# Output projection: x's and v's products in one item, m1's and m2's late additions with y, and tile halves normalised on VectorE and ScalarE

## The chip, the cores and the metric

The kernel runs on one core of a Trainium2 chip. The metric is the device time of one execution in microseconds; several runs are given by their median, lowest and highest. The profile is one execution taken by the hardware profiler. In its rows PE is TensorE (PEld its weight loads), DVE is VectorE, ACT is ScalarE, POOL is GpSimd and SP the engine that issues most DMAs; L1160 is line 1160 of the kernel. A time like 574.58 is counted in microseconds from the start of the span.

## The reference, cut to what matters

Two layers, each a token mixer of three gated branches, one output projection, a residual addition with a layer norm, and then a SwiGLU feed-forward block (FFN) with a second residual and norm. The changed code is the output projection with its norm (`ln1`), and the norm's step that is also used between the two layers (`ln2` of the first):

```
    for l in range(DEPTH):                        # 2
        h = jnp.einsum('bsd,de->bse', x, w_in[l])
        ...
        mix = jnp.einsum('bsd,de->bse', merged, w_out[l])
        x = _layer_norm(DEEPNORM_ALPHA * x + mix, ln1_g[l], ln1_b[l])

        u = jnp.einsum('bsd,df->bsf', x, w_ffn_in[l])
        u_gate, u_up = jnp.split(u, 2, axis=-1)
        ffn = jnp.einsum('bsf,fd->bsd', jax.nn.silu(u_gate) * u_up, w_ffn_out[l])
        x = _layer_norm(DEEPNORM_ALPHA * x + ffn, ln2_g[l], ln2_b[l])
```

x is 512 rows by 1024 columns, w_out 1024 by 1024, everything in float32.

## The kernel before

**Numbers as pairs.** A float32 value is carried as a high and a low part (names that end in `h` and `l`, or `wh` and `wl` for weights). One product is three matmuls (`mm3`, L122 to L124): high by high, high by low, low by high. ACT makes the high part with a cast (L106, or L282 for a weight block), DVE the low part with a subtraction (L112, or L283).

**Weights.** A block of weights comes by DMA into a buffer `st` (SP's queue, or POOL's at L178), is cast to `wh` by ACT (L282) and split by DVE (L283, `wl`). There are three buffers of `wh` and `wl`, and the program prepares blocks up to three ahead of the item that uses them.

**Items.** The program is a list of items `(specs, fn, groups...)`: `specs` are the weight blocks, `fn` issues the products on PE and what follows them, and each group is a list of small functions that is run between the steps of the item's `fn`. The text order of the items, and of what is prepared ahead, gives a first order; a scheduler places each engine's instructions, so the order on an engine is not quite that of the text. Each engine runs its own queue in that order, and waits where an instruction's input isn't there.

**The output projection** (`out_items`) computes the 512 x 1024 by 1024 x 1024 product by a seven-product scheme on halves: the products are named m1, m2, y, v, x, g and h, each on sums of halves of the activations (`m2h`, `s12h`, `s43h`) and on sums of blocks of the weight, which the class `Late` builds with DVE additions in place (L271, `e += d`, builds the block of h). Each product has two row tiles (`j` 0 and 1). Several products share a bank of PSUM: x, g and h go on accumulating in m1's, v in y's. So a product that goes on in a bank can start only when DVE has read what the bank held.

**Residual tiles.** The residual stands in SBUF as row tiles of 128 rows in two halves of 512 columns, `z[t][hf]`. `plus` adds a bank's contents to a half: the first time with the residual's factor (L1160), then plainly (L1162); after the last of a half come the statistics (`stats`, L489, BN_STATS). m1's and m2's additions are kept in a list `late` and run in v's item. When both halves are whole, `normalise` (L504) computes mean and variance (BN_AGGR, L506), adds eps (L508), raises to the power -1/2 on POOL (L509) and applies both to the two halves on DVE (L511).

**The transposes.** The FFN needs the normalised rows turned: PE transposes the halves into banks `px` (L529, or L520 at the layer boundary), ACT evacuates each with scale and shift (L545, to `xf`), casts it to `xTh` (L106), and DVE makes `xTl` (L112). The first FFN products (`pf`) run between them.

`normalise` is used at three places: in the out-projection of layer 0 (from about 580 us), at the layer boundary behind the first FFN (930 to 945 us) and in the out-projection of layer 1 (from about 1510 us). The end of the last layer uses another function (`finish`).

`bcast_rows` (L476) loads ln1's scale and shift rows into tiles `bc` on SP's queue; it is called by `norm_rows`, a group of x's item.

Of the kernel before, what the change touches and what calls it, by code (L numbers as in the profile page):

```python
# [12 lines left out]
F32 = mybir.dt.float32  # L13
F32R = mybir.dt.float32r
AF = mybir.ActivationFunctionType
ALU = mybir.AluOpType

P = 128
# [38 lines left out]
def trunk(ctx, tc, x_in, xT_in, w_in, ret_norm_g, da_norm_g, lq1, lk1, lq2, lk2, w_a, w_b, w_c, b_merge, w_out,  # L57
          ln1_g, ln1_b, w_ffn_in, w_ffn_out, ln2_g, ln2_b, rel, rope_ret, rope_da, decay, out):
    nc = tc.nc
    ctx.enter_context(nc.allow_low_precision("float32 operands are carried exactly as pairs of float32r"))  # L60
    cpool = ctx.enter_context(tc.tile_pool(name="cpool", bufs=1))
    small = ctx.enter_context(tc.tile_pool(name="small", bufs=6))
# [128 lines left out]
    class Chain(Halves):  # L191
# [15 lines left out]
        def x(self):  # L207
            return self.take(1, 0)
# [4 lines left out]
        def v(self):  # L213
            return self.block(self.load(1, 1))
# [147 lines left out]
    def product(acts, name, j, wt, ps=None):  # L362

        onto, sl = ps is not None, slice(P * j, P * j + P)
        ps = ps if onto else bank("pf")
        for k in range(wt.nk):
            hi, lo = acts[k].use[name]
            mm3(ps, hi[:, sl], lo[:, sl], wt.hi[:, k], wt.lo[:, k], k == 0 and not onto, k == wt.nk - 1, onto)
        return ps
# [109 lines left out]
    class Norm:  # L479
# [24 lines left out]
        def normalise(self, t):  # L504
            mv = small.tile([P, 2], F32, tag="mv", name="mv")
            nc.vector.bn_aggr(mv, self.st[t])  # L506
            rs = small.tile([P, 1], F32, tag="rs", name="rs")
            nc.vector.tensor_scalar_add(rs, mv[:, 1:2], LN_EPS)  # L508
            nc.gpsimd.tensor_tensor(rs, rs, mhalf[:, 0:1], op=ALU.pow)  # L509
            for z in self.z[t]:  # L510
                nc.vector.tensor_scalar(z, z, mv[:, 0:1], rs[:, 0:1], op0=ALU.subtract, op1=ALU.mult)  # L511

        def transposes(self, t):
            hf, j = divmod(t, 2)
# [49 lines left out]
    def between():  # L564

        if pending:
            for fn in pending.pop(0):
                fn()
# [58 lines left out]
    def layer(l):  # L627
# [7 lines left out]
        v = {}  # L635
# [64 lines left out]
        def u_rqk(dst, base, hp):  # L700
            def fn(wt):
                for j in range(2):
                    rqk_done(dst, 2 * hp + j, proj_T(xT, wt, P * j))
                    between()
            return [([wcols(base + 256 * hp, 256)], KT)], fn
# [87 lines left out]
        def s_dh(h):  # L793
            def fn():
                dhs[h] = g(name="dh")
                nc.sync.dma_start(dhs[h], decay[h])
            return fn

        def s_r1(h):
            def fn():  # L800
                dh = dhs.pop(h)
                rp[h] = triangle("rp")
                q, k = rq.pop(h), rk.pop(h)
                for b in range(3):
                    tmp = g(name="rtmp")
                    for mt in range(NT):
                        if PACK[mt][0] != b:
                            continue
                        o, w = PACK[mt][1], S - P * mt
                        ps = bank("psr")  # L810
                        msl = slice(P * mt, P * mt + P)
                        mm3(ps[:, :w], k.hi[:, msl], k.lo[:, msl], q.hi[:, P * mt:], q.lo[:, P * mt:], True, True)
                        nc.vector.tensor_mul(tmp[:, o:o + w], ps[:, :w], dh[:, :w])
                    w = PACKW[b]
                    split(rp[h][b], tmp[:, :w], cols=slice(0, w))
            return fn
# [37 lines left out]
        def s_r3(h):  # L854
            def fn():
                os_ = rps.pop(h)
                for d in range(2):
                    ps = bank("prt")
                    for nt in range(NT):
                        nc.tensor.transpose(ps[:, P * nt:P * nt + P],  # L860
                                            os_[nt // 2][:, 256 * (nt % 2) + P * d:256 * (nt % 2) + P * d + P], ident)
                    oa[2 * h + d] = Pair("oa")
                    split(oa[2 * h + d], ps, scale=v["rg"][:, d:d + 1])
            return fn
# [30 lines left out]
        def u_cqk(p):  # L895
            def fn(wt):
                cqk[p] = QK()
                cqk[p].set_q(proj_T(xT, wt, 0), -CA_DH ** -0.5)
                between()
                cqk[p].set_k(proj_T(xT, wt, P))  # L900
            return [([wcols(CQ + P * p, P), wcols(CK + P * p, P)], KT)], fn
# [173 lines left out]
        def u_gate(br, i):  # L1075
            def fn(wt):
                for j, d in enumerate(tiles(br, i)):
                    gate_done(br, d, proj_T(xT, wt, P * j), (br, i) in EARLY)
                    between()
            return [(cols_of(W, GATE + D * br, br, i), KT)], fn  # L1080
# [39 lines left out]
        def s_mleft(k):  # L1120
            def fn():
                mq[k].left(acc[k], acc[k + 4], 0.5)
            return fn

        def s_mright(k):
            def fn():
                mq[k].right(acc.pop(k), acc.pop(k + 4), 0.5)
            return fn
# [44 lines left out]
        def out_items():  # L1173

            hv = Late(w_out[l], 0, 4)
            w = {}
            late = []

            def it(name, i, hf, op, last=False, whole=False):
                def fn(wt):  # L1180
                    on = {"x": "m1", "g": "m1", "h": "m1", "v": "y"}.get(name, name)
                    for j in range(2):
                        t = 2 * i + j
                        ps = w[on, j] = product(mq, name, j, wt, w.pop((on, j), None))
                        add = functools.partial(plus, x1, t, hf, ps, op, last)
                        if name in ("m1", "m2"):
                            late.append(add)
                        else:
                            add()
                        if name == "v":  # L1190
                            for fn in late[j::2]:
                                fn()
                        if whole:
                            x1["n"].normalise(t)
                        between()
                return [getattr(hv, name)], fn

            add, sub = ALU.add, ALU.subtract
            return {"c": hv.ahead_c, "a": hv.ahead_a, "m1": it("m1", 0, 0, add), "m2": it("m2", 0, 0, add, True),
                    "y": it("y", 1, 1, add), "x": it("x", 0, 1, sub, True, True), "v": it("v", 0, 1, add), "g": it("g", 1, 1, sub, True),  # L1200
                    "h": it("h", 1, 0, add, True, True)}

        def s_turned(hf):
# [7 lines left out]
        o = out_items()  # L1211
# [15 lines left out]
        for (specs, fn), *groups in start + [  # L1227
            (w["x"], [p["a"]]), (u_gate(0, 3),), (w["g"],), (w["h"], [p["c"]]),
            (p["m1"], [s_dh(0)]), (p["y"], [], [s_r1(0)]), (p["v"], [s_dh(1)]), (p["m2"], [], [s_r1(1)]),
            (p["x"], [q["a"]]), (u_rqk(rq, RQ, 1),), (p["g"], [q["c"]]), (p["h"],),  # L1230
            (q["m1"], [], [s_r2(0)]), (q["y"], [s_r2(1)]), (u_rqk(rk, RK, 1), [], [s_r3(0)]),
            (q["v"], [s_dh(2)], [s_r3(1)]), (q["m2"], [], [s_r1(2)]), (q["x"], [s_dh(3)]), (u_cqk(0),), (q["g"], [], [s_r1(3)]), (q["h"],),
            (u_gate(2, 0), [s_r2(2)], [s_r2(3), s_r3(2)]), (u_cqk(1), [s_r3(3)] + c(0)[0], c(0)[1]),
            (u_branch(0, 0), c(1)[0] + [v_back(cv)], c(1)[1]), (u_branch(0, 1), *c(2)), (u_cqk(2), *c(3)),
            (u_branch(0, 2), *c(4)), (u_cqk(3), *c(5)), (u_branch(0, 3), *c(6)), 
            (u_dqk(0), [s_c3(5), s_c2(6)], [s_c1(7)]), (u_gate(1, 0), [s_c3(6)], [s_c2(7)]),
            (u_dqk(1), [v_back(dv), s_c3(7)] + d(0)[1]), (u_branch(1, 0), *d(1)),
            (u_gate(1, 1), [], d(2)[1]), (u_branch(1, 1), [s_d2(0)], d(3)[1]), (u_dqk(2), [s_d3(0)]),
            (u_gate(1, 2), *d(4)), (u_branch(1, 2), *d(5)), (u_dqk(3),),
            (u_gate(1, 3), *d(6)), (u_branch(1, 3), *d(7)), (u_gate(2, 1), [gates_in(2, 0), s_d4(2)], [s_d2(3)]),  # L1240
            (u_gate(2, 2), [s_d3(3)], [rows_in, s_d4(3)]),
            (u_branch(2, 0), [o["a"]], [s_mleft(0)]), (u_branch(2, 1), [], [s_mleft(1)]), (u_gate(2, 3), [s_mright(0)], [s_mright(1), o["c"]]),
            (u_branch(2, 2),), (u_branch(2, 3), [], [s_mleft(2), s_mleft(3)]),
            (o["m1"], [s_mright(2)]), (o["m2"], [s_mright(3)]), (o["y"],), (o["v"],), (o["x"], [norm_rows]),
            (o["g"], [], [s_turned(0)]), (o["h"],),
        ]:
            item(specs, fn, *groups)
# [168 lines left out]
        o, w = fout_items(0), fout_items(1)  # L1416
# [68 lines left out]
```

## Time and profile before

| | |
|---|---|
| median of 3 runs | 1878.59 us (1877.79 to 1879.77) |
| profiled execution | 1878.62 us, its span 1876.8 us |
| granted clock of TensorE | 0.999 of full speed |
| instructions | 23329 in the span |
| DMA | 302.89 MB, mean 161 GB/s |

The page gives the busy time of each engine, its share of the span and the number of instructions; PE's is 99%. The list of waits of PE names what it stood still for. A timeline row has the start, the duration, the engine, the line, the operation, output and inputs, the shape, how many instructions the row joins, and in brackets the idle time before it and what ended it. The durations of matmuls are those of a pipeline (0.39 us), while the next one starts 0.23 us later.

### The profile page before, as it was taken

The numbers are of one execution on the slowest core, as the hardware profiler recorded it, in microseconds if no ns is written. First come the engines' busy times: TensorE is split into PE (matmuls) and PEld (weight loads), VectorE is DVE, ScalarE is ACT, GpSimd is POOL, SyncE is SP. The second block draws the span as 40 slices with busy tenths as digits, with TensorE's granted clock in tenths as the row PEclk, the third lists the DMA queues.
The fourth block names the chain that finished last, engine by engine and source line by source line (L and its number), as shares of the span: only waits on it lengthen the run. The fifth ranks groups of instructions, "written<-read, shape, count | busy, mean of one in ns | idle before, by whom it ended". The sixth has DMA issues, their size and how long they took to land. (4 is left out here: it accounts for less than half of the span.)

```text
span 1876.8 us, 23329 instructions
## 1 busy us (share of the span) xinstructions
PE 1857.4 (99%) x8754; PEld 1543.6 (82%) x8754; DVE 1395.9 (74%) x2121; ACT 989.2 (53%) x1593; POOL 127.2 (7%) x149
## 2 busy tenths in 40 slices
PE   9999999999999999999999999999999999999998
PEld 7788888888887888888878888888888878888886
DVE  6777766677679777888687777567775887778886
ACT  5555555576544545554264555556665454455541
POOL 2000000000000000010020000000000001000100
PEclk9999999999999999999999999999999999999999
DMA  9585444332456577697376844433325467777871
GB/s 288 164 268 161 118 138 138 90 124 78 122 159 180 157 186 192 189 224 201 130 229 191 253 116 144 153 116 95 112 68 146 136 178 177 197 196 203 202 193 45
DMA packets 235937, 302.89 MB, mean 161 GB/s; under 512 B 8756, under 2 KB 127632, under 8 KB 235824
## 3 DMA queue, kind: packets, MB, share of 16 engines
q1 hardware_dynamic: 207600, 246.44, 40.5%
q0 software_dynamic: 28224, 54.95, 16.9%
q8 instruction: 69, 1.13, 0.2%
q14 instruction: 44, 0.36, 0.1%
HBM read 279.29 MB, written 22.07 MB: 161 GB/s over the span
## 5 line engine op out<-in xcount | busy, mean ns | idle before, releaser
L283 DVE TENSOR_TENSOR wl<-st,wh 128x2048 fp32r<-128x2048 f32 x140 | 320.1, 2289 | 118.0 <-ACT wh L282 117.4
L282 ACT CAST wh<-st 128x2048 fp32r<-128x2048 f32 x140 | 267.1, 1912 | 234.8 <-PE pf L124 114.2
L122 PE MATMUL pt<-xTh,wh 128*128 128x512 f32 x960 | 377.9, 394 | 2.0 <-ACT wh L154 1.3
L123 PE MATMUL pt<-xTl,wh 128*128 128x512 f32 x960 | 373.9, 389 | 0.2 <-DVE xTl L613 0.2
L124 PE MATMUL pt<-xTh,wl 128*128 128x512 f32 x960 | 374.1, 390 | 0.0
L155 DVE TENSOR_TENSOR wl<-st,wh 128x1024 fp32r<-128x1024 f32 (+1 forms) x188 | 200.7, 1084 | 52.3 <-ACT wh L154 38.5
L154 ACT CAST wh<-st 128x1024 fp32r<-128x1024 f32 (+1 forms) x188 | 172.6, 941 | 109.5 <-PE pt L123 56.3
L122 PEld LDWEIGHTS pt<-xTh,wh 128*128 128x128 f32 x960 | 180.5, 188 | 40.0 <-ACT wh L154 2.4
L124 PEld LDWEIGHTS pt<-xTh,wl 128*128 128x128 f32 x960 | 180.2, 188 | 38.1
L123 PEld LDWEIGHTS pt<-xTl,wh 128*128 128x128 f32 x960 | 180.4, 188 | 36.7 <-DVE xTl L613 0.5
L122 PE MATMUL pf<-wh,xTh 128*128 128x512 f32 x336 | 133.4, 398 | 1.6 <-ACT xf L545 0.5
L123 PE MATMUL pf<-wl,xTh 128*128 128x512 f32 x336 | 131.1, 390 | 0.0
L124 PE MATMUL pf<-wh,xTl 128*128 128x512 f32 x336 | 130.2, 392 | 0.0
L122 PE MATMUL pf<-wh,s43h 128*128 128x512 f32 x256 | 100.2, 392 | 1.7 <-DVE z L1162 1.7
L123 PE MATMUL pf<-wl,s12h 128*128 128x512 f32 x256 | 100.0, 391 | 1.2 <-DVE wl L283 1.2
L122 PE MATMUL pf<-wh,s12h 128*128 128x512 f32 x256 | 100.1, 394 | 0.0
L123 PE MATMUL pf<-wl,s43h 128*128 128x512 f32 x256 | 99.7, 389 | 0.0
L124 PE MATMUL pf<-wh,s12l 128*128 128x512 f32 x256 | 99.4, 390 | 0.0
L124 PE MATMUL pf<-wh,s43l 128*128 128x512 f32 x256 | 99.0, 389 | 0.0
L757 ACT COPY tc<-pf 128x512 f32<-128x512 f32 x84 | 48.5, 590 | 80.2 <-PE pf L124 75.0
L122 PEld LDWEIGHTS pf<-wh,xTh 128*128 128x128 f32 x336 | 63.1, 188 | 18.4 <-ACT xf L545 2.4
L124 PEld LDWEIGHTS pf<-wh,xTl 128*128 128x128 f32 x336 | 62.6, 188 | 15.3 <-DVE xTl L112 2.7
(328 smaller groups left out, 3661.8 us busy)
## 6 DMA issues: line engine op xcount, KB each, us to landing
st<-in_w_in SPq DMA_DIRECT2D x53, 1024.0 KB, 6.4
st<-in_w_ffn_in SPq DMA_DIRECT2D x38, 1024.0 KB, 5.5
st<-in_w_in SPq DMA_DIRECT2D x48, 512.0 KB, 4.7
st<-in_w_ffn_in POOLq DMA_DIRECT2D x20, 1024.0 KB, 10.8
st<-in_w_ffn_out SPq DMA_DIRECT2D x20, 1024.0 KB, 7.8
st<-in_w_ffn_out POOLq DMA_DIRECT2D x16, 1024.0 KB, 8.7
st<-in_w_in POOLq DMA_DIRECT2D x12, 1024.0 KB, 10.9
st<-in_w_out SPq DMA_DIRECT2D x12, 1024.0 KB, 5.1
```

The lines of the kernel that those rows point to most:

```text
L122: nc.tensor.matmul(ps, lh, rh, start=start, stop=False, skip_group_check=onto)
L123: nc.tensor.matmul(ps, lh, rl, start=False, stop=False, skip_group_check=onto)
L124: nc.tensor.matmul(ps, ll, rh, start=False, stop=stop, skip_group_check=onto)
L154: return [nc.scalar.copy(self.hi[:, a:b], self.st[:, a:b]), nc.vector.tensor_sub(self.lo[:, a:b], self.st[:, a:b], f(self.hi[:, a:b]))]
L155: nc.vector.tensor_sub(self.lo[:, a:b], self.st[:, a:b], f(self.hi[:, a:b]))]
L282: nc.scalar.copy(self.hi, st)
L283: nc.vector.tensor_sub(self.lo, st, f(self.hi))
L757: nc.scalar.copy(t[to, j], ps)
```

## The change

Three edits in the same function and one helper.

- `normalise` now computes `nb` = -mean * rs on DVE (128x1), applies the first half on ACT as rs * z + nb (an ACTIVATE with scale and bias from tiles), and the second on DVE as before.
- The list `late` runs in y's item instead of v's.
- x and v are one item, `xv`: its two weight blocks are prepared together, it issues x's products and then v's. The last product of a half on columns 512 to 1023 of rows 0 to 255 is now v's, so statistics and `normalise` follow v. `norm_rows` moves to this item's third group.

```diff
             nc.gpsimd.tensor_tensor(rs, rs, mhalf[:, 0:1], op=ALU.pow)
-            for z in self.z[t]:
-                nc.vector.tensor_scalar(z, z, mv[:, 0:1], rs[:, 0:1], op0=ALU.subtract, op1=ALU.mult)
+            nb = small.tile([P, 1], F32, tag="nb", name="nb")
+            nc.vector.scalar_tensor_tensor(nb, mv[:, 0:1], -1.0, rs, op0=ALU.mult, op1=ALU.mult)
+            z = self.z[t]
+            nc.scalar.activation(z[0], z[0], AF.Identity, scale=rs[:, 0:1], bias=nb[:, 0:1])
+            nc.vector.tensor_scalar(z[1], z[1], mv[:, 0:1], rs[:, 0:1], op0=ALU.subtract, op1=ALU.mult)
...
-                        if name == "v":
+                        if name == "y":
                             for fn in late[j::2]:
                                 fn()
...
+            x, v = it("x", 0, 1, sub)[1], it("v", 0, 1, add, True, True)[1]
+
+            def xv(wv, wx):
+                x(wx)
+                v(wv)
+
             return {"c": hv.ahead_c, "a": hv.ahead_a, "m1": it("m1", 0, 0, add), "m2": it("m2", 0, 0, add, True),
-                    "y": it("y", 1, 1, add), "x": it("x", 0, 1, sub, True, True), "v": it("v", 0, 1, add), "g": it("g", 1, 1, sub, True),
+                    "y": it("y", 1, 1, add), "xv": ([hv.v, hv.x], xv), "g": it("g", 1, 1, sub, True),
                     "h": it("h", 1, 0, add, True, True)}
...
-            (o["m1"], [s_mright(2)]), (o["m2"], [s_mright(3)]), (o["y"],), (o["v"],), (o["x"], [norm_rows]),
+            (o["m1"], [s_mright(2)]), (o["m2"], [s_mright(3)]), (o["y"],), (o["xv"], [], [], [norm_rows]),
```

In the changed kernel the lines below `normalise` stand three further: L1163 and L1165 are the additions (L1160 and L1162 before), L532 the transposes (L529), L548 the evacuation (L545). Inside it L511 is `nb`, L513 ACT's half, L514 DVE's half.

**DVE, behind v's and x's products of layer 0.** z_4786 to z_4793 are the halves of row tiles 0 to 3 (two each), pf_5108 and pf_5128 m1's banks, pf_5187 and pf_5201 y's. Before:

```order
L1160 SCALAR_TENSOR_TENSOR z_4787<-z_4787,pf_5187 128x512
L1160 SCALAR_TENSOR_TENSOR z_4789<-z_4789,pf_5201 128x512
L1162 TENSOR_TENSOR z_4787<-z_4787,pf_5108 128x512
L1162 TENSOR_TENSOR z_4789<-z_4789,pf_5128 128x512
L283 TENSOR_TENSOR wl_5253<-st_5181,wh_5252 128x2048
L489 BN_STATS bn_4802<-z_4787 128x6
L489 BN_STATS bn_4803<-z_4789 128x6
L506 BN_AGGR mv_5270<-bn_4802 128x2
L283 TENSOR_TENSOR wl_5309<-st_5306,wh_5308 128x2048
L508 TENSOR_SCALAR rs_5272<-mv_5270 128x1
L506 BN_AGGR mv_5299<-bn_4803 128x2
L1162 TENSOR_TENSOR z_4791<-z_4791,pf_5108 128x512
```

After:

```order
L1165 TENSOR_TENSOR z_4787<-z_4787,pf_5187 128x512
L271 TENSOR_TENSOR st_5148<-st_5148,st_5141 128x2048
...
L506 BN_AGGR mv_5265<-bn_4802 128x2
L489 BN_STATS bn_4803<-z_4789 128x6
L508 TENSOR_SCALAR rs_5267<-mv_5265 128x1
L283 TENSOR_TENSOR wl_5307<-st_5148,wh_5306 128x2048
L511 SCALAR_TENSOR_TENSOR nb_5270<-mv_5265,rs_5267 128x1
L514 TENSOR_SCALAR z_4787<-z_4787,mv_5265,rs_5267 128x512
L506 BN_AGGR mv_5296<-bn_4803 128x2
L283 TENSOR_TENSOR wl_5313<-st_5310,wh_5312 128x2048
L508 TENSOR_SCALAR rs_5298<-mv_5296 128x1
L1165 TENSOR_TENSOR z_4791<-z_4791,pf_5108 128x512
```

The additions that read m1's banks (pf_5108) for x stand ahead of these rows now. L271, which builds h's block, stood above the first of the rows before and now follows v's first addition; the first `nb` and DVE's half of tile 0 stand ahead of the addition that frees pf_5108 for h. Two rows are left out.

**ACT at the layer boundary.** xf_7924 to xf_7942 before and xf_7938 to xf_7956 after are the first evacuations, z_6881 is the first half of row tile 2. Before:

```order
L545 ACTIVATE xf_7930<-px_7865,colv_348 128x256
L106 CAST xTh_7928<-xf_7930 128x256
L545 ACTIVATE xf_7936<-px_7866,colv_348 128x256
L106 CAST xTh_7934<-xf_7936 128x256
L282 CAST wh_8000<-st_7998 128x2048
L545 ACTIVATE xf_7942<-px_7866,colv_348 128x256
L154 CAST wh_8005<-st_8004 128x1024
L106 CAST xTh_7940<-xf_7942 128x256
```

After:

```order
L548 ACTIVATE xf_7944<-px_7875,colv_348 128x256
L106 CAST xTh_7942<-xf_7944 128x256
L513 ACTIVATE z_6881<-z_6881,nb_7932,rs_7929 128x512
L548 ACTIVATE xf_7950<-px_7876,colv_348 128x256
L106 CAST xTh_7948<-xf_7950 128x256
L282 CAST wh_8016<-st_8014 128x2048
L548 ACTIVATE xf_7956<-px_7876,colv_348 128x256
L154 CAST wh_8021<-st_8020 128x1024
L106 CAST xTh_7954<-xf_7956 128x256
```

ACT's half of tile 2 stands between the second cast and the third evacuation; the weight cast and the fourth evacuation follow it.

## The prediction

> **What bounds the kernel now.** I read the page first, then the waits of PE, then the timelines of PE, DVE, ACT and POOL around the three places where `normalise` is called. The columns of part 1 are busy time, share of the span and count.
>
> ```profile
> PE 1857.4 (99%) x8754; PEld 1543.6 (82%) x8754; DVE 1395.9 (74%) x2121; ACT 989.2 (53%) x1593; POOL 127.2 (7%) x149
> PE pf L122 <- DVE rs L508: 2.6, 2, 1.3
> PE pf L122 <- DVE z L1162: 1.7, 2, 0.8
> PE pf L123 <- DVE wl L283: 1.2, 2, 0.6
> ```
>
> TensorE sets the time: it is busy for 99% of the span, and the change neither adds nor removes a matmul. So the change can save only time in which PE stands still, and can cost only where it makes PE stand still. The three rows of waits (total, times, longest) are the ones that lie in the out-projection, once in each layer; they sum to 5.5 us, and no forecast of a gain can be much above that. In the timeline of layer 0 they look like this (start, us, engine, then the wait in brackets):
>
> ```profile
> 570.53 0.40 PE L123 MATMUL pf<-wl,s12h 128*128 128x512 f32 x1
> 571.54 0.50 PE L123 MATMUL pf<-wl,s12h 128*128 128x512 f32 x1 [0.61 <-DVE wl L283]
> ...
> 582.47 0.39 PE L124 MATMUL pf<-wh,s12l 128*128 128x512 f32 x1
> 583.70 0.50 PE L122 MATMUL pf<-wh,s43h 128*128 128x512 f32 x1 [0.84 <-DVE z L1162]
> ...
> 586.10 0.39 PE L123 MATMUL pf<-wl,s43h 128*128 128x512 f32 x1
> 586.33 0.39 PE L124 MATMUL pf<-wh,s43l 128*128 128x512 f32 x1
> ...
> 589.05 0.39 PE L124 MATMUL pf<-wh,s43l 128*128 128x512 f32 x1
> 590.78 0.47 PE L122 MATMUL pf<-wh,m2h 128*128 128x512 f32 x1 [1.34 <-DVE rs L508]
> ```
>
> An undisturbed step from start to start is 586.33 - 586.10 = 0.23 us. The first step of item g (operand s43h) comes 1.23 us after the last of v and x, so PE loses 1.00 there; the first of h (m2h) comes after 1.73, a loss of 1.50; the early one, at 571.54, is 1.01 after its predecessor and loses 0.78.
>
> **What DVE does there** decides the first two, since g and h accumulate onto banks that DVE must have read before:
>
> ```profile
> 574.58 2.27 DVE L271 TENSOR_TENSOR st<-st 128x2048 f32<-128x2048 f32 x1
> 581.76 1.28 DVE L1160 SCALAR_TENSOR_TENSOR z<-z,pf 128x512 f32<-128x512 f32 x2 [0.83 <-PE pf L124]
> 582.96 1.28 DVE L1162 TENSOR_TENSOR z<-z,pf 128x512 f32<-128x512 f32 x2
> 584.16 2.28 DVE L283 TENSOR_TENSOR wl<-st,wh 128x2048 fp32r<-128x2048 f32 x1
> 587.66 2.24 DVE L283 TENSOR_TENSOR wl<-st,wh 128x2048 fp32r<-128x2048 f32 x1
> 589.82 0.14 DVE L508 TENSOR_SCALAR rs<-mv 128x1 f32<-128x1 f32 x1
> 590.00 0.63 DVE L1162 TENSOR_TENSOR z<-z,pf 128x512 f32<-128x512 f32 x1
> ```
>
> g starts right behind the addition of 582.96 that frees m1's first bank; h starts behind the addition of 590.00, which stood behind a subtraction of 2.24 us that nothing on PE needed yet.
>
> **Part one, the late additions with y.** By the order of the two kernels, DVE adds m1's and m2's first products at the same places in both. This edit moves nothing: 0.0.
>
> **Part two, x ahead of v in one item.** PE has already issued x's first products ahead of v's in the kernel before (s12h at 570.53), and the early wait on wl stays. What changes is DVE: the addition of x that reads m1's bank comes before v's products are done, about 574.8 instead of 582.96. g no longer waits: it starts at 582.47 + 0.23 = 582.70, a gain of 1.00 per layer. What it costs stands in the same queue: `e += d` (L271, 2.27 us), which ran at 574.58 in cover of x's and v's products, now stands behind v's first addition (580.2 to 580.8), and the block of h is built from it:
>
> - L271 ends at 580.8 + 2.27 = 583.1; ACT's cast of that block (1.91, the row of L282 in the timeline below) at 585.0; its L283 (2.28) at 587.3.
> - The power of `normalise` on POOL is issued at 585.1, beside that subtraction. These are the two forms it has in the trace, alone and beside a subtraction:
>
> ```profile
> 934.92 0.54 POOL L509 TENSOR_TENSOR rs<-rs,mhalf 128x1 f32<-128x1 f32 x1 [4.66 <-DVE rs L508]
> 943.16 1.21 DVE L155 TENSOR_TENSOR wl<-st,wh 128x1024 fp32r<-128x1024 f32 x1
> 943.39 1.39 POOL L509 TENSOR_TENSOR rs<-rs,mhalf 128x1 f32<-128x1 f32 x1 [7.93 <-DVE rs L508]
> ```
>
> It ended 0.41 behind the subtraction (943.39 + 1.39 less 943.16 + 1.21), so I let it end at 587.7. Then nb (0.16, from L1036 below) to 587.9, DVE's half tile (0.54) to 588.4, the next L283 (2.28) to 590.7, and only then the addition of g (0.68) to 591.4. h starts at 591.45, 0.67 later than before, although g ended 1.00 earlier.
>
> [...]
>
> **Part three, the halves on two engines.** Of each tile one DVE instruction goes and one ACTIVATE with two pointer operands comes, and a 128x1 instruction (nb) on DVE that must wait for POOL. For their durations (count, total and mean ns, then idle):
>
> ```profile
> L511 DVE TENSOR_SCALAR z<-z,mv,rs x24: 535/541/547, 594.6 to 1537.4; 128x512 f32<-128x512 f32 x24
> L1036 DVE SCALAR_TENSOR_TENSOR ss<-ss,sums x8: 161/164/165, 439.3 to 1449.7; 128x4 f32<-128x4 f32 x8
> L106 ACT CAST s43h<-sb 128x512 fp32r<-128x512 f32 x16 | 9.9, 620 | 24.5 <-DVE sb L316 24.5
> L106 ACT CAST cP<-ptr 128x256 fp32r<-128x256 f32 x16 | 6.2, 388 | 0.0
> L545 ACT ACTIVATE xf<-px,colv 128x256 f32<-128x256 f32 x48 | 25.9, 576 | 22.1 <-PE px L529 11.3 <-PE px L520 10.8
> ```
>
> ACT has no such instruction before. An ACT pass over 128x512 from SBUF is 0.62 (s43h); two pointers add 576 - 388 = 188 ns at 128x256; so I take 0.81. The lower bound is 0.62; the upper is the 0.62 scaled by 576/388, 0.92, and I go to 1.0. DVE's 12 halves less are 12 x 0.54 = 6.5 us of DVE work, off the path; of the page DVE idles for a quarter. [...]
>
> In the out-projection, four transposes now stand on PE ahead of h. They need ACT's half (587.9 to 588.8) and take about 0.5 us, in time that PE spends waiting for h anyway and that the later stretch saves. The waits among the later transposes come to about 1.2 in the walk instead of 1.4. So each out-projection, counted from h's start, which has g's gain in it already: +0.67 (h) - 0.5 (transposes done early) - 0.2 = **about 0.0**, in both layers.
>
> **The DMAs that move.** `norm_rows` now comes with xv, and the first power stands ahead of POOL's DMA:
>
> ```profile
> 577.34 1.26 SPq L476 DMA_DIRECT2D bc<-in_ln_g  x2
> 580.39 15.83 SPq L150 DMA_DIRECT2D st<-in_w_ffn_in  x6
> 590.20 1.29 POOL L178 DMA_DIRECT2D st<-in_w_ffn_in  x1 [58.60 <-DVE mv L506]
> ```
>
> The four loads of ln1's rows go out some 8 us earlier on SP, and the FFN blocks behind them 2 to 3 later, because the buffer that they wait for comes free later; they land by 584 and 591, ahead of their casts at 590 and after. POOL's DMA is issued behind a power that waits for DVE, 0.9 later, and lands (8.6 us) 0.9 later. In the walk no row of PE waits for any of the three: 0.0. If that cover were gone, each would cost its 0.9 to 2.8 once per layer.
>
> At the layer boundary ACT carries the evacuations (L545), the casts to xTh (L106) and the weight casts, close behind each other:
>
> ```profile
> 934.76 0.56 ACT L545 ACTIVATE xf<-px,colv 128x256 f32<-128x256 f32 x1
> 935.35 0.41 ACT L106 CAST xTh<-xf 128x256 fp32r<-128x256 f32 x1
> 936.33 1.91 ACT L282 CAST wh<-st 128x2048 fp32r<-128x2048 f32 x1 [0.57 <-PE pf L124]
> 938.15 0.55 ACT L545 ACTIVATE xf<-px,colv 128x256 f32<-128x256 f32 x1
> 939.55 0.40 ACT L106 CAST xTh<-xf 128x256 fp32r<-128x256 f32 x1
> 940.21 0.40 PE L122 MATMUL pf<-wh,xTh 128*128 128x512 f32 x1
> ```
>
> The half of tile 2 is queued ahead of the third evacuation. It needs the power (ended 935.46, now about 935.86, since the queue before it is longer) and nb; it runs from 936.1 to 936.9 (ACT's own queue holds it no longer than that). The third L545 moves from 934.76 to 936.8, the weight cast from 936.33 to 937.74, the fourth xTh from 939.55 to 941.00, ready at 941.4. Before, PE's first step that reads it ran at 940.21 without waiting; in the new order PE has other products until about 940.8: a wait of about 0.7 that wasn't there. Going on through ACT's queue, one lo half (xTl, DVE behind ACT) comes 0.8 late where it came 0.0; the other waits (0.5 and 0.4) stay. 0.7 + 0.8, and 0.1 on the next item's first product: **+1.6**.
>
> **Sum.** 0.0 + 0.0 + 1.6 = +1.6 against the profiled execution: span 1876.8 + 1.6 = 1878.4, and 1878.62 - 1876.80 = 1.82 lie around it: 1880.2. The median of the runs shown, 1878.59, is the same to 0.03. With the ACT half at 0.62 the same walk through the queues gives +1.2, at 1.0 it gives +2.8, at 1.3 +5.5; nb at 0.13 gives +1.3, at 0.25 +2.1.
>
> **Rivals.** What a measurement of this kernel can tell from no change is about 0.2%, 3.8 us: faster is below 1874.8, slower above 1882.4.
>
> *Both waits go.* If g's gap vanishes and the longer DVE queue ahead of h is covered too, each layer gains 1.00 + 1.50 = 2.5, 5.0 in both, and with nothing on ACT that is 1873.6. For it: DVE has 6.5 us less to do. Against it: L271 leaves its cover, and an addition that frees h's bank still stands behind two subtractions of 2.28. 0.10.
>
> *ACT becomes the bound behind the transposes* (slower). In each of the three places the halves of tiles 2 and 3 stand among the evacuations of the first transposes, where ACT's idle time before its weight cast was 0.57. If these six halves show on PE in full, that is 6 x 0.81 = 4.9, 1883.5; the same comes from a half of 1.2 us. It decides from about 1.1 us a half, or from five of the six being uncovered. For it: ACT is in order, and the half waits for POOL and DVE with evacuations behind it; a hold-up that the page cannot show (an added wait between three engines for each tile) adds to it. Against it: 22.1 us of idle time before L545, most of it slack of ACT. 0.35.
>
> *It does nothing.* PE ran x ahead already and the late additions did not move; if ACT's half hides at the boundary too, the time stays at 1878.6. For it: PE is 99% busy. Against it: the fourth xTh, done at 939.95, was read at 940.21, and PE's other products cover only about 0.6 more of the 1.4 that it is late. 0.13.
>
> The forecast itself has 0.42. Same is 0.42 + 0.13 = 0.55, faster 0.10, slower 0.35. The likeliest alone spans 1878.8 to 1882. The range goes up to 1884.4 for the ACT rival (a half of 1.3 us gives 1884.1), and down to 1877.2: the idle case at the boundary, with h no later than before in both layers (2 x -0.7 on 1878.6). What lies outside is most of the first rival and the far end of the second.
>
> **What would show it.** Right: g's first product starts 0.23 after v's last; the wait in front of h names a later DVE row and is about 2 us, with 4 transposes ahead of it; ACT's half takes 0.8; between the first transposes of the layer boundary and the next item's first product PE loses 1.5 us more than before. Wrong: an ACT half over 1.1, a power that holds up nb for more than a microsecond at every tile, DMA waits of the moved weight load at the head of the FFN, or h without any wait.

## The result and the profile after

| | before | after |
|---|---|---|
| median | 1878.05 us (1877.54 to 1880.07, 14 runs) | 1882.85 us (1880.60 to 1884.99, 14 runs) |
| ratio | | 1.0021, 95% interval 1.0014 to 1.0028 |
| profiled execution, span | 1878.62, 1876.8 us | 1883.15, 1881.4 us |
| granted clock in it | 0.999 | 0.997 |

The change makes the kernel slower, by 4.8 us in the medians; 1880.2 was forecast, with a range up to 1884.4. The runs also spread further than before: 4.4 us instead of 2.5.

The first part of the page of the changed kernel, and the first rows of what PE waited for (us in total, times, longest):

```profile
PE 1860.0 (99%) x8754; PEld 1546.1 (82%) x8754; DVE 1393.1 (74%) x2121; ACT 997.5 (53%) x1605; POOL 131.7 (7%) x149
PE pf L122 <- DVE z L1165: 3.8, 2, 1.9
PE pf L122 <- ACT xTh L106: 1.7, 4, 0.6
...
PE px L532 <- ACT z L513: 1.2, 2, 0.6
PE pf L123 <- DVE wl L283: 1.2, 2, 0.6
...
PE pf L124 <- DVE xTl L112: 0.7, 2, 0.6
```

PE's count of matmuls is the same and it is busy 2.6 us longer (1857.4 before): the same matmuls took longer somewhere. Waits alone don't explain the difference. To see where it arose, I marked five points on PE's timeline, the same in each kernel: the early wait on `wl` in each out-projection (571.54 and 1504.07 before) and the first product of the item behind it or behind the layer boundary. In the profile of the changed kernel these rows are:

```profile
571.35 0.50 PE L123 MATMUL pf<-wl,s12h 128*128 128x512 f32 x1 [0.60 <-DVE wl L283]
612.75 0.39 PE L122 MATMUL pt<-xTh,wh 128*128 128x512 f32 x1
953.50 0.39 PE L122 MATMUL pt<-xTh,wh 128*128 128x512 f32 x1
1505.89 0.50 PE L123 MATMUL pf<-wl,s12h 128*128 128x512 f32 x1 [0.60 <-DVE wl L283]
1549.94 0.39 PE L122 MATMUL pt<-xTh,wh 128*128 128x512 f32 x1
```

Before, the three later `pt` rows stand at 612.92, 951.66 and 1545.42. That gives three stretches:

| stretch | before | after | difference | forecast |
|---|---|---|---|---|
| out-projection, layer 0 | 41.38 | 41.40 | +0.02 | 0.0 |
| first FFN and layer boundary | 338.74 | 340.75 | +2.01 | +1.6 |
| out-projection, layer 1 | 41.35 | 44.05 | +2.70 | 0.0 |

What is left of the spans' 4.6 lies outside these stretches and sums to -0.2. The two out-projections run the same instructions, and the change gave one of them 0.02 and the other 2.70.

**Layer 1.** PE's timeline of the changed kernel ahead of h, and the granted clock in stretches of 4 us (stretch, its length, PE's busy time and matmuls, PEclk, DMA share, GB/s):

```profile
1522.38 0.39 PE L124 MATMUL pf<-wh,s43l 128*128 128x512 f32 x1
1523.38 0.66 PE L532 MATMUL px<-ident,z 128*128 128x128 f32 x4 [0.61 <-ACT z L513]
1525.93 0.80 PE L122 MATMUL pf<-wh,m2h 128*128 128x512 f32 x1 [1.89 <-DVE z L1165]
1526.52 0.63 PE L123 MATMUL pf<-wl,m2h 128*128 128x512 f32 x1
1526.95 0.63 PE L124 MATMUL pf<-wh,m2l 128*128 128x512 f32 x1
...
1532.05 0.40 PE L124 MATMUL pf<-wh,m2l 128*128 128x512 f32 x1
1532.29 0.40 PE L122 MATMUL pf<-wh,m2h 128*128 128x512 f32 x1
```

```profile
1520.00:1524.00 4.00, 3.39 (x17) 1.00 0.85 231
1524.00:1528.00 4.00, 2.11 (x6) 0.65 0.89 227
1528.00:1532.00 4.00, 4.00 (x11) 0.50 1.06 183
1532.00:1536.00 4.00, 4.00 (x25) 1.00 1.12 274
```

The waits are those of the forecast: 0.6, then four transposes, then 1.9. What follows them was in no term: the matmuls of h start 0.43 us apart instead of 0.23, until 1532, and in that time the clock that TensorE was granted is half. The clock is 0.50 from 1525.20 to 1532.03, 6.83 us. In layer 0 of the same execution the same stretch kept its clock, 1.00 from 584 to 624:

```profile
587.85 0.39 PE L124 MATMUL pf<-wh,s43l 128*128 128x512 f32 x1
588.86 0.66 PE L532 MATMUL px<-ident,z 128*128 128x128 f32 x4 [0.62 <-ACT z L513]
591.40 0.50 PE L122 MATMUL pf<-wh,m2h 128*128 128x512 f32 x1 [1.88 <-DVE z L1165]
591.73 0.39 PE L123 MATMUL pf<-wl,m2h 128*128 128x512 f32 x1
```

So one drop costs 44.05 - 41.40 = 2.65 us. **Theory A** was: the boundary costs 2.0, and the quiet stretch ahead of h (2.5 us of waits around 0.66 us of transposes, where the kernel before has one wait of 1.3 us) lets the clock fall in part of the executions, in either layer. Rivals: B, the low clock comes by chance; C, the waits alone make the loss; D, ACT's halves make it; E, the order of x and v makes it.

### The profile page after: what moved, and what is told of

It reads as the page before. It is cut to its first block, busy times and chain, and to the rows that moved or that the text cites. A ratio compares the mean times of both kernels' runs of the same rounds, so it can differ in the third digit from the quotient of the medians.

```text
span 1881.4 us, 23327 instructions
## 1 busy us (share of the span) xinstructions
PE 1860.0 (99%) x8754; PEld 1546.1 (82%) x8754; DVE 1393.1 (74%) x2121; ACT 997.5 (53%) x1605; POOL 131.7 (7%) x149
## 5 line engine op out<-in xcount | busy, mean ns | idle before, releaser
L283 DVE TENSOR_TENSOR wl<-st,wh 128x2048 fp32r<-128x2048 f32 x140 | 320.1, 2289 | 115.8 <-ACT wh L282 115.1
```

What stands on the lines that cost most here:

```text
L283: nc.vector.tensor_sub(self.lo, st, f(self.hi))
```

## The experiments

The kernel before has a median of 1878.1 to 1878.3 in each group of runs. "Stretches" are the three of the table above, in its order, from the profiled execution. Where an edit adds or takes lines, the numbers behind it move by a few, so the operation and the names tell which step a row is: L285 below is L283 of the changed kernel, L533 and L534 are its L532, and L1164 and L1166 its L1165.

**Twelve more transposes ahead of h.** Nothing else differs from the changed kernel, and the bank gets the same values.

```diff
-                    nc.tensor.transpose(ps[:, o:o + P],
-                                        self.z[2 * hf + j][k // 4][:, P * (k % 4):P * (k % 4) + P], ident)
+                    for _ in range(4 if hf == 0 and j == 0 and k == 2 * b else 1):
+                        nc.tensor.transpose(ps[:, o:o + P],
+                                            self.z[2 * hf + j][k // 4][:, P * (k % 4):P * (k % 4) + P], ident)
```

> The changed kernel, with each of the four transposes that stand ahead of h issued four times instead of once (same bank, same values): 12 more instructions on PE in each out-projection, about 1.5 us of PE work inside h's wait of 1.9 us. Theory A, the clock: in the changed kernel's profile TensorE's granted clock is 0.50 for 6.83 us behind this quiet stretch of layer 1, which costs about 2.9 us each time it happens. With PE busy there the clock stays at 1.00, h starts where it started, and the time falls in spite of the added work: about 1880.8 (median of the changed kernel 1882.85), spans within about 1 us of each other. Theory B, the low clock comes by chance and not from the idle stretch: 1882.9 or more, with the same spread as the changed kernel. Theory C, the waits alone make the whole loss: 1882.9.

Measured: 1880.05 (1879.15 to 1881.75, 11 runs), ratio 1.0009, interval 1.0000 to 1.0017; clock 0.999 in 8 of 11 runs and 0.998 in the others, where the changed kernel had 0.999 in 2 of 14. A mean of 0.998 can come from the end of the kernel alone, where the clock falls behind the last matmul, in the kernel before to 0.50 at 1873.42 of 1876.8 us (the profile of the new normalise alone, below, has 0.998 and no other drop); 0.997 or less came in 8 of 14 runs of the changed kernel, in 2 of 35 of the kernel before and in none of these. Stretches 41.38, 340.76, 41.41. In its timeline:

```profile
1522.98 1.97 PE L533 MATMUL px<-ident,z 128*128 128x128 f32 x16 [0.60 <-ACT z L513]
1525.52 0.50 PE L122 MATMUL pf<-wh,m2h 128*128 128x512 f32 x1 [0.57 <-DVE z L1166]
```

h starts 20.06 us behind the mark (1525.52 - 1505.46), in the changed kernel 20.04 (1525.93 - 1505.89). The added work cost nothing, and with it the median fell by 2.8 us. That is what A expects (1880.8 was expected); B and C expected 1882.9. The rest, 1.9, is the boundary.

**Four more instead of twelve** (each twice).

> The changed kernel with each of the four transposes ahead of h issued twice: 4 more instead of 12, about 0.5 us of PE work, which leaves 0.6 and some 1.4 us idle. If the clock goes by the work in a stretch of 3.4 us, the drops become rarer than in the changed kernel and not as rare as with four times: median between 1880.1 and 1882.8, about 1881. If one long idle piece decides (over some 1.5 us), they go wholly: 1880.1. If the four-fold transposes helped in another way than by PE's work: 1882.8.

Measured: 1880.25 (1879.57 to 1882.28, 11 runs), ratio 1.0011, 1.0003 to 1.0020. Four of its runs lie above 1881.5 (one of eleven with the twelve), the rest where the twelve had them. The profiled execution is the highest of the four, 1882.28, and its clock did not fall ahead of the kernel's end: stretches 41.42, 340.79 and 41.40. Its early mark stands 2.2 us later than with the twelve (573.13 against 570.93), so what it has too much arose ahead of that mark (last section). The clock of the runs is 0.997 in one of the eleven and 0.998 or 0.999 in the others. So half a microsecond of PE work in the middle of the stretch takes most of the drops away, although the wait ahead of h is still long:

```profile
1527.76 0.50 PE L122 MATMUL pf<-wh,m2h 128*128 128x512 f32 x1 [1.45 <-DVE z L1166]
```

Of the other three, 1881.71 is the run with 0.997; whether the two others had a drop isn't known. The median is too near to that of the twelve to tell the first expectation from the second.

**The idle stretch without the change.** To the kernel before, two idle reads of each bank of g were added:

```diff
+                        if name == "g":
+                            jk = small.tile([P, 6], F32, tag="jk", name="jk")
+                            for _ in range(2):
+                                nc.vector.bn_stats(jk, ps)
                         if name in ("m1", "m2"):
```

> The kernel before with nothing of the change, but each of g's two banks read by two idle instructions on DVE (BN_STATS into a tile that nothing uses, 0.69 us each) ahead of g's additions. h then waits some 1.8 us longer: about 3.3 us without any work on PE, where the kernel before has 1.5. Theory A, an idle stretch drops the clock: +1.8 per layer for the wait, and behind it 3.4 or 6.8 us at 0.50 in each layer, 1.5 to 2.9 us each: about 1886, clock 0.996 or lower in every run, though neither ACT's halves nor the order of x and v are in it. Theory B, the low clock belongs to something else in the changed kernel: 1878.2 + 3.6 = 1881.8, clock 0.999.

Measured: 1883.62 (1882.79 to 1885.35, 6 runs), ratio 1.0029, 1.0017 to 1.0040; clock 0.997 in every run. Stretches 43.38, 338.82, 43.69.

```profile
592.25 0.76 PE L122 MATMUL pf<-wh,m2h 128*128 128x512 f32 x1 [3.19 <-DVE z L1162]
```

```profile
588.00:592.00 4.00, 1.05 (x5) 0.97 1.07 257
592.00:596.00 4.00, 3.75 (x19) 0.61 1.06 169
596.00:600.00 4.00, 4.00 (x20) 1.00 0.68 139
```

The drop came in both layers of the profiled execution, with none of the change's code in the kernel: B is out. The size was too high (1886): h started 1.9 later, as expected, but the stretches grew by 2.0 and 2.3 only. DVE's halves now stand ahead of the last addition of g, so the transposes came early and no longer waited; the half clock, only 3.41 us long here, began at 591.73 in layer 0, 0.52 ahead of h, so part of it fell into the wait.

**Order without the new normalise**, and **new normalise without the order** (two kernels, each with one half of the diff).

> The change without its new normalise: x and v in one item and the late additions with y, but both halves on DVE. Theory A (layer boundary 2.0 us for ACT's half, the clock for the rest): the boundary is as before (338.7 us between the marks instead of 340.8), the out-projections still have four transposes and a wait of about 2 us ahead of h (two halves of 0.54 on DVE instead of one and nb), so clock drops remain in part of the runs: about 1881, spread of some 3 us. Theory D, ACT's halves make the whole loss: 1878.0. Theory E, the order of x and v makes the whole loss: 1882.9.

> The kernel before with the new normalise alone: first half on ACT, nb on DVE. Theory A: the layer boundary gets its 2.0 us; the out-projections keep the gaps of before (1.0 ahead of g, 1.5 ahead of h, no transposes between), too short for the clock to drop: 1880.0, clock 0.999 in every run, spread within 1.5 us. Theory D, ACT's halves make the whole loss: 1882.9. Theory E: 1878.0.

| | median, runs | ratio, interval | clock of the runs | stretches |
|---|---|---|---|---|
| order only | 1881.60 (1879.53 to 1884.90), 11 | 1.0018, 1.0010 to 1.0027 | 0.995 to 0.998 | 43.37, 338.74, 43.33 |
| normalise only | 1879.90 (1879.20 to 1880.04, and one of 1887.19), 12 | 1.0010, 1.0001 to 1.0018 | 0.998 and 0.999, one 0.997 | 41.26, 340.71, 41.26 |

The losses are apart: the order costs only in the out-projections, the new normalise only at the boundary. 1881.6 - 1878.2 = 3.4 and 1879.9 - 1878.2 = 1.7 sum to 5.1, against 4.7. In the kernel with the order alone both layers drop in the profiled execution, so ACT's half is not needed for it; two halves of 0.54 on DVE ahead of g's addition make the wait even longer:

```profile
591.58 0.47 PE L122 MATMUL pf<-wh,m2h 128*128 128x512 f32 x1 [2.58 <-DVE z L1162]
```

The one run of 1887.19 (clock 0.997) has no profile, and its cause isn't known. D and E each explain only their half. With the new normalise alone the out-projections even gain 0.1 each (41.26).

**Old normalise at the boundary alone**, in the changed kernel, and **half of it** in the kernel with the new normalise alone (row tiles 2 and 3 on DVE there).

```diff
-        def normalise(self, t):
+        def normalise(self, t, split=True):
...
+            if not split:
+                for z in self.z[t]:
+                    nc.vector.tensor_scalar(z, z, mv[:, 0:1], rs[:, 0:1], op0=ALU.subtract, op1=ALU.mult)
+                return
...
-                        n.normalise(t)
+                        n.normalise(t, False)
```

The second has `t < 2` in place of `False`.

> The changed kernel with the old normalise (both halves on DVE) at the layer boundary alone. Theory A: the boundary's 2.0 us go, the out-projections and their clock drops stay: 1880.9, with a spread of 3 us and more. Theory E, the order makes the whole loss: 1882.9. Theory D: 1878.0 or somewhat above.

> The kernel before with the new normalise, but at the layer boundary its ACT half for row tiles 0 and 1 only; tiles 2 and 3 have both halves on DVE. If the boundary's cost comes from tile 2's half standing on ACT ahead of the third evacuation (the prediction's step), the wait for xTh at 941, the one for xTl at 947 and the later ones go; what stays is the 0.3 that the first transposes wait for tile 1's half: 339.0 us between the marks instead of 340.7, and 1878.4. If the switch to ACT costs wherever it stands: 340.7 and 1879.9.

The first: 1880.00 (1878.11 to 1882.54, 11 runs), ratio 1.0010, 1.0001 to 1.0018; stretches 42.88, 338.81, 41.39. The boundary's 2.0 are gone, and in the profiled execution the clock dropped in layer 0 this time and not in layer 1 (+1.5 for a drop of 3.4 us). The second: 1878.53 (11 runs), ratio 1.0002, 0.9992 to 1.0011; stretches 41.30, 339.21, 41.24. Of the boundary's 2.0 three quarters go with tiles 2 and 3, as the step on the third evacuation says; 0.5 stay, of which this row shows 0.3:

```profile
927.27 1.09 PE L527 MATMUL px<-ident,z 128*128 128x128 f32 x8 [0.30 <-ACT z L517]
```

**h's block summed earlier**, in the changed kernel:

```diff
+        def add_e(self):
+            nc.vector.tensor_add(self.e, self.e, self.__dict__.pop("d"))
+
         def h(self):
-            nc.vector.tensor_add(self.e, self.e, self.__dict__.pop("d"))
             return self.block(self.__dict__.pop("e"))
...
                 x(wx)
+                hv.add_e()
                 v(wv)
```

> The changed kernel with h's block summed (e += d) between x's and v's products instead of at h's preparation: L271 stands ahead of v's first addition again, where x's and v's products cover it. If L271's lost cover is what makes h late, h starts about 2 us earlier than in the changed kernel, the clock stays up and the time is 1879.5 to 1880. If the queue of subtractions, nb and half tile ahead of g's addition makes it (theory A's walk), h starts only 0.4 to 0.6 earlier, and the quiet stretch and the drops stay: about 1882.

Measured: 1884.23 (1883.07 to 1885.78, 6 runs), ratio 1.0033, 1.0021 to 1.0045; stretches 42.63, 340.68, 42.71. Neither expectation held. L271 stands ahead of v's first addition again, but that moved it little: it starts 8.68 us behind the mark, in the changed kernel 9.34 and in the kernel before 3.04. So what its old place is worth isn't tested here. DVE's subtractions ran 0.3 and 1.4 us earlier, but both now stand ahead of `nb`, and PE has the four transposes ahead of h:

```profile
588.67 2.24 DVE L285 TENSOR_TENSOR wl<-st,wh 128x2048 fp32r<-128x2048 f32 x1
591.37 0.16 DVE L513 SCALAR_TENSOR_TENSOR nb<-mv,rs 128x1 f32<-128x1 f32 x1 [0.47 <-POOL rs L511]
```

```profile
592.58 0.66 PE L534 MATMUL px<-ident,z 128*128 128x128 f32 x4 [2.75 <-ACT z L515]
592.99 0.48 PE L122 MATMUL pf<-wh,m2h 128*128 128x512 f32 x1
```

Now the transposes wait 2.75 us for ACT's half and h not at all: h starts 20.07 behind the mark, as in the changed kernel (20.05). DVE's addition that frees h's bank came 0.27 earlier; the transposes' place ahead of h, with `nb` behind both of DVE's subtractions, holds h just as long. The clock did not fall in this execution ahead of the kernel's end. The 1.2 us by which the stretch of layer 0 is longer than the changed kernel's 41.40 lie behind h: the waits listed there sum to 0.8 us instead of 0.5, and the rest isn't traced to a row.

**No transposes ahead of h.** The order of x and v and the late additions stay, the sum of h's block as in the last kernel, normalise as before on DVE, but for tiles 0 and 1 behind g's additions:

```diff
-                        if whole:
+                        if whole and name != "v":
                             x1["n"].normalise(t)
+                        if name == "g" and j == 1:
+                            x1["n"].normalise(0)
+                            x1["n"].normalise(1)
```

> x and v in one item, late additions with y, e += d between x and v, the old normalise on DVE, and normalise of tiles 0 and 1 moved behind g's additions (no transposes ahead of h). Theory A: g has no wait (1.0 per layer gained), h waits some 1.4 us and starts 1.0 earlier than before, clock 0.999; half of the gain may go again to later transposes, which wait for the halves: 1876.2 to 1877.2 against 1878.1 before. If the order of x and v itself costs: 1880 or more.

> The same kernel as best1, a second time on another occasion: by the first (1876.19 against 1878.2, interval of the ratio 0.9983 to 1.0001) and by its marks (40.3 us in each out-projection instead of 41.4) it should be 2 us faster again: 1876.2 with the kernel before at 1878.2. If the first was chance: within 0.5 us of before.

| | median, runs | before beside it | ratio, interval | stretches |
|---|---|---|---|---|
| first | 1876.19 (1875.52 to 1877.66), 11 | 1878.20 | 0.9992, 0.9983 to 1.0001 | 40.32, 338.74, 40.37 |
| again | 1877.50 (1875.46 to 1878.09), 11 | 1878.14 | 0.9993, 0.9984 to 1.0002 | 40.27, 338.74, 40.34 |

The stretches are 1.0 to 1.1 shorter in each layer in both profiled executions, and g has no wait:

```profile
590.97 0.47 PE L122 MATMUL pf<-wh,m2h 128*128 128x512 f32 x1 [1.62 <-DVE z L1164]
```

The gain is the 1.00 per layer that the prediction priced for g, here without the transposes ahead of h: h starts 0.74 earlier behind the mark (18.50 against 19.24), and the rest is gained behind it. The sum of h's block has moved as well, so the gain isn't that of the order of x and v alone. The ratio of the runs agrees with some 1.4 us, but its interval reaches just over 1 both times, and the second median gained 0.6 where 2 were expected; why the runs fall into two groups stands in the last section. It is faster by its stretches; by the runs' ratio alone it isn't settled.

**The same with ACT's halves in the out-projections.**

> As the kernel of the row above (x and v in one item, e += d between, normalise behind g's additions), with the first half on ACT in the out-projections and on DVE at the layer boundary. If DVE's queue between g's additions and the transposes is what holds, the ACT half frees 0.4 us per tile there: 1875.7 to 1877; if the wait for POOL, nb and ACT costs as much as it frees: equal to the other within 0.5 us.

Measured: 1880.47 (1879.32 to 1882.31, 11 runs), ratio 1.0010, 1.0002 to 1.0019; stretches 42.00, 338.89, 42.00: 1.7 slower in each layer than with DVE alone, which neither expectation allowed. The first products behind the transposes wait:

```profile
600.75 0.50 PE L122 MATMUL pf<-wh,xTh 128*128 128x512 f32 x1 [1.33 <-ACT xTh L106]
```

With both halves on DVE the same row waits 0.94. That is 0.4 of the 1.7; waits for `xTl` add another 0.4 there, and where the rest lies isn't shown.

## Why the prediction was right, and where it was not

- **Part one, late additions:** 0.0. The out-projection of layer 0 came out at +0.02, which fits; no kernel had this edit alone, so it isn't shown by itself.
- **Part two, g's gain of 1.00 and h's loss:** right in mechanism. g has no wait; h starts 0.81 later behind the mark than before (20.05 against 19.24; 0.67 forecast); POOL's power took 2.72 us beside the subtraction; DVE's rows of the walk (L271 at 580.8, `nb` at 587.9, the addition at 590.7) came within 0.2:

```profile
580.69 2.28 DVE L271 TENSOR_TENSOR st<-st 128x2048 f32<-128x2048 f32 x1
585.03 2.29 DVE L283 TENSOR_TENSOR wl<-st,wh 128x2048 fp32r<-128x2048 f32 x1
587.79 0.16 DVE L511 SCALAR_TENSOR_TENSOR nb<-mv,rs 128x1 f32<-128x1 f32 x1 [0.47 <-POOL rs L509]
588.45 2.24 DVE L283 TENSOR_TENSOR wl<-st,wh 128x2048 fp32r<-128x2048 f32 x1
590.67 1.27 DVE L1165 TENSOR_TENSOR z<-z,pf 128x512 f32<-128x512 f32 x2
```

```profile
585.04 2.72 POOL L509 TENSOR_TENSOR rs<-rs,mhalf 128x1 f32<-128x1 f32 x1 [53.44 <-DVE rs L508]
```

  The power started at 585.04 and ended at 587.76, 0.44 behind the subtraction; 587.7 was taken from the row of the kernel before, where it ended 0.41 behind.
- **Part three, ACT's half:** 0.81 was taken, and the twelve of them took 0.815 each:

```profile
L513 ACT ACTIVATE z<-z,nb,rs 128x512 f32<-128x512 f32 x12 | 9.8, 815 | 22.8 <-DVE nb L511 22.8
```

- **The DMAs that move:** 0.0 was forecast; PE's list of waits has no new wait for a weight block in the changed kernel, and layer 0's out-projection is as long as before.
- **The layer boundary:** +1.6 was forecast, +2.01 came. The mechanism was the one told, tile 2's half ahead of the third evacuation, which came at 936.73 (936.8 forecast); the wait for xTh was 0.55 (0.7 forecast) and for xTl 0.56 (0.8). Not seen were the 0.3 that the first transposes wait for tile 1's half, and 0.2 on the later ones (`px`, DVE's half). The four rows sum to 1.62, and the other 0.4 is in none of them:

```profile
927.79 1.09 PE L523 MATMUL px<-ident,z 128*128 128x128 f32 x8 [0.29 <-ACT z L513]
941.28 0.50 PE L122 MATMUL pf<-wh,xTh 128*128 128x512 f32 x1 [0.55 <-ACT xTh L106]
947.08 0.50 PE L124 MATMUL pf<-wh,xTl 128*128 128x512 f32 x1 [0.56 <-DVE xTl L112]
947.80 1.31 PE L532 MATMUL px<-ident,z 128*128 128x128 f32 x10 [0.22 <-DVE z L514]
```

- **The sum** lacked a term. "About 0.0, in both layers" counted each wait at its length and set g's gain off against h's loss as if idle time had the same price wherever it stands. It had not: g's 1.00 and h's 1.50 were two short pieces 7 us apart, and the change drew them together into one quiet stretch of 3.2 us with 0.66 us of transposes in it. The clock that TensorE is granted fell behind it in part of the executions, 2.65 us for a drop of 6.8 us and 1.5 for one of 3.4. Twelve idle transposes in that stretch took 2.8 us off the median, and what is left of 4.8 is the boundary. The prediction's own steps gave what they forecast where the clock stayed up: 0.0 against +0.02 in layer 0.
- **The rivals:** the slower side had 0.35, for another reason (ACT behind the transposes in all three places). ACT's queue did cost, at one place of three. The median came out just above its bound for slower, 1882.4, and not for that rival's cause. So it was luck that the range held the time: its upper part was there for ACT's halves, and the clock was in no term and no rival. "Both waits go" did not happen; the kernel without the early transposes shows that g's half of it can be had.

## What to carry to other kernels

Price idle time of TensorE by where it lies, not by its sum: two short waits apart may be cheaper than one quiet stretch of the same length, since the granted clock fell behind the latter here. In the profiled executions the drops, to 0.50, followed quiet stretches with 2.5 us of waits or more, and the two that could be priced cost 1.5 and 2.65 us. Look at the granted clock in short windows behind the longest waits, and if a wait can't be removed, try idle matmuls in it: twelve idle transposes ahead of each h took 2.8 us off the median here. Before a step is moved off a queue, look at what it covered and at what the scheduler puts in front of the next product: here a normalise that came earlier brought transposes ahead of h, and with them a chain over three engines.

## What the runs showed of the hardware

**The granted clock fell to half behind quiet stretches, for 3.41 us or for 6.83.** Six drops ahead of the kernel's end were seen in the profiled executions: one in the changed kernel, two with the order alone, one with the old normalise at the boundary and two with the idle reads. Five lasted 3.41 us, and the changed kernel's 6.83 us. In the 3.41 us ahead of the drop, PE had been busy 0.48, 0.24, 0.41, 0.37, 0.21 and 0.07 of the time, in this order, so it had not stood still all the while in any of the six. In the first 3.41 us at half clock PE was busy 0.79 of the time in the changed kernel and 0.85 to 1.00 in the other five.

Not every quiet stretch was followed by a drop. In layer 0 of the changed kernel PE was busy 0.91 of the 3.41 us from 588.10 on, a share of 0.27, and the clock was 1.00 there and up to 624; in layer 1 it fell behind 1.64 us of work in 3.41. With h's block summed earlier, PE was busy 1.43 of the 4 us from 590 on and 1.55 of the 4 us from 1524 on, and the clock was 1.00 there and in the 4 us behind. So why one layer of the changed kernel kept its clock and the other did not isn't shown by these executions, nor how much work would have been enough.

**The start of the kernel comes in two kinds.** The same kernel (the one without transposes ahead of h) was profiled twice, with spans of 1875.7 and 1874.5; the early mark stands at 572.47 in one and 571.28 in the other, so all of the 1.2 arose ahead of it. Between 8 and 12 us from the start PE ran 14 matmuls in the first and 19 in the second:

```profile
8.00:12.00 4.00, 4.00 (x14) 1.00 1.13 303
```

```profile
8.00:12.00 4.00, 4.00 (x19) 1.00 1.07 317
```

The column of the clock says 1.00 in both, and yet the pace differs. In the first execution matmuls start 0.43 us apart until 10.5 us, the pace of h's matmuls at half clock above, and 0.23 apart from then on; the second has 19 between 8 and 12 us, as many as in the 4 us behind. What makes the first slow isn't shown. Two rows of the first:

```profile
9.19 0.63 PE L123 MATMUL pt<-xTl,wh 128*128 128x512 f32 x1
9.62 0.63 PE L124 MATMUL pt<-xTh,wl 128*128 128x512 f32 x1
```

By the early mark the 13 profiled executions fall into two groups. In four (the first of this kernel, the one with four more transposes, the one with h's block summed earlier, and the last one above, with ACT's halves in the out-projections) it stands at 572.47 to 573.13. In the other nine it stands at 570.93 to 571.54. The matmuls of the start are known for eleven: in three of the four the slow pace lasts until 10.5 to 11.0 us, and in eight of the nine the full pace is there by 8 us. For the one with four more transposes and the one with tiles 2 and 3 on DVE only the mark is known.

The runs of this kernel fall into two groups, 1875.5 to 1876.3 and 1877.5 to 1878.1, and those of the kernel before in the first group of experiments into 1877.0 to 1878.7 and 1879.5 to 1880.6 (35 runs). How many of the few runs fall into which moves a median by more than the gain, so medians a microsecond apart say little here, and the stretches between marks more. The profiled executions fit this: of this kernel the slow start took 1877.47 us and the other 1876.23, the kernel before took 1878.62 with full pace by 8 us, and the one with four more transposes 1882.28 with a late mark. That the groups of the other runs come from the two starts is argued from these.
